# Output-gate block 4 between head 2's value tiles, and two branch projections behind the gates of block 2

## The chip, the core and the metric

One core of one Trainium2 chip runs the whole kernel in one launch. The metric is device time in microseconds, from the start of the program to its end. Engines are named as the profile names them: PE is TensorE (matmuls; PEld its weight loads), DVE is VectorE, ACT is ScalarE, POOL is GpSimd, SP is SyncE, which issues most of the DMAs.

## The reference, cut to what matters

The block is a residual layer on 512 tokens of width 1024 with two branches and a feed-forward part. What bears on the change:

```python
att = _forgetting_attention(fq, fk, fv, ff)              # 8 heads x 64
u  = silu(causal_conv(mu))                               # per channel, width 4
mq = einsum('bshi,hik->bshk', uh, w_mq)                  # 4 heads, qk 128
mk = einsum('bshi,hik->bshk', uh, w_mk)
hm = _mlstm_chunkwise(mq, mk, mv, mi, mf)                # v 256 for each head
hm = _head_norm(hm, mh_norm_g) * sigmoid(mo)
y  = sigmoid(ga) * (att @ w_pa) + sigmoid(gb) * (hm @ w_pb)
return y @ w_out
```

`mu`, `mv`, `mo`, `ga` and `gb` are column blocks of one input projection `h @ w_in + b_in`; `h` is the normalised and modulated input. Behind this come a LayerNorm, a SwiGLU feed-forward and a second LayerNorm.

## The kernel before

**Numbers.** Every fp32 product is made of three matmuls on fp32r halves (`mm3`, lines 184, 187 and 188): a value is split into `hi` (a cast on ACT, line 191) and `lo` (value minus `hi`, on DVE, line 192). Weights come in chunks in the order of `plan()`, are cast on ACT (line 155) and subtracted on DVE (line 159); `get(key)` asks for a chunk and starts the loads of the next three. Chunks pass through a ring of three raw buffers and a ring of four for the halves.

**Projections.** A block of 128 output columns, transposed, is 24 matmuls of 512 columns into one PSUM bank (`gemm_fm`); it is a generator that yields half-way and at its end. What empties the bank depends on the block: for `mo` a tanh on ACT (line 321) and a scaling on DVE (line 322) into a tile of the pool `mlb` for blocks 2 to 7; for `ga` and `gb` a tanh (line 583) into a tile of `mla` for block 0 and of `hml` for the others.

**PSUM.** Eight banks in four rings of two: `acc` (projections, value tiles, `mqk`), `s` (scores, `pa`, `pb`), `tr` (transposes), `o` (`fo` of the attention, `mn` of the mLSTM).

**The attention** (`fox_scores`, `fox_out`) runs over four pairs of heads. For each block `kb` of keys of a pair it transposes the weights (`ft`, line 661), ACT copies them out (`pT`, line 663), and `fo` (line 669) sums into a bank of the ring `o`; then `atthi` and `attlo` (lines 687, 688) empty it.

**The mLSTM** runs over four heads. `prep(h)` makes the values: four tiles of 128 tokens (`mv`, 24 matmuls of 256 columns each), each emptied by DVE into `vt` (line 612, one buffer) and split into `vxh` and `vx`; then `mqk`, from which queries and keys are copied. The tile `vxh` stands in a ring of two in the pool `adap`, tag `adaw`, which the loads of the modulation weights (`ada_load`) share. `ml_scores(h)` loads a row broadcast (`nb`, on ACT's queue, line 702), forms four weight tiles (E, line 707; a mask on POOL; the scores `ms`, line 710; a product on DVE, line 711; a split). `ml_num(h, tb)` sums `tb + 1` products into a bank of the ring `o` (`mn`, line 722), takes statistics and normalises into `hn` (lines 724 to 736). Two transposes per group (`mt`, line 755) fill two `tr` banks, and line 761 multiplies them with `mo` into `hm`.

**The order.** Work is written down in one sequence, and a planner at build time fixes each engine's order: earlier lines first, but what is ready by its own reckoning goes ahead of what isn't. A pool opened where another closed takes its memory, so its tiles wait for the old pool's last use: `mlb` is opened where `fox` closes (line 690), `hml` where `mlb` closes (line 763). Around the heads, `queue` holds generators (projections, `prep`), and `fill(n)` takes the next n steps of it. In the loop over heads, `fill(2)` stands behind the scores, `fill(1)` before each of the later groups, and two more at the last. A step is half a block, one value tile, or `mqk`.

**Behind the heads.** `hm` is split block by block into `hmhi` and `hmlo` (tiles of `hml`). Then, for f = 0 to 7: the gates `ga` and `gb` of block f (those of block 0 were made before), `pa` of block f (12 matmuls, emptied by line 792 into the gate's tile) and `pb_block(f - 1)` (24 matmuls on `hmhi` and `hmlo`, emptied by lines 778 and 780), whose result is split into `yhi` and `ylo`. From block 2 on, each gate projection is preceded by three `ada_block`s, a load and a reduction of modulation weights each.

Of the kernel before, what the change touches and what calls it, by code (L numbers as in the profile page):

```python
# [8 lines left out]
F32 = mybir.dt.float32  # L9
# [7 lines left out]
P = 128  # L17
D = 1024
S = 512
# [16 lines left out]
VW = TB * 258  # L36
# [6 lines left out]
def plan():  # L43
    out = [("start", k) for k in range(KT)]
    out += [("gv", j) for j in range(4)]

    def mu(h):
        return [("mu", 2 * h), ("mu", 2 * h + 1)]

    def mvqk(h):  # L50
        return [("mv", 2 * h), ("mv", 2 * h + 1), ("mqk", h)]

    out += mvqk(0)
    out += [("fq", 2), ("fk", 2)]
    out += mu(1) + mvqk(1)
    out += [("fq", 3), ("fk", 3)]
    out += mu(2)
    out += [("mo", 0), ("mo", 1)]
    out += mu(3)
    out += [("mo", 2), ("mo", 3)]  # L60
    out += mvqk(2)
    out += [("mo", 4), ("mo", 5)]
    out += mvqk(3)
    out += [("mo", 6), ("mo", 7)]
    for f in range(8):
        out += [("ga", f), ("gb", f), ("pa", f)]
        if f > 0:
            out += [("pb", f - 1)]
    out += [("pb", 7)]
    out += [("wo", k) for k in range(KT)]  # L70
    for f in range(FT):
        out += [("fg", f), ("fu", f)]
    for q in range(4):
        out += [("dn", q * 6 + j) for j in range(6)]
    return out
# [15 lines left out]


PLAN = plan()
POOL_LO = [("start", 0)]
LATE_LO = [(n, f) for f in range(3) for n in ("fg", "fu")]
# [3 lines left out]
def block_kernel(ctx, tc, x, c, wada, wpk, cols, gvb, mvb, lnp, out):  # L99
# [77 lines left out]
    def get(key, ahead=AHEAD):  # L177
        prefetch(key, ahead)
        return st["tiles"].pop(key)

    def mm3(ps, lhs, rhs, first, last, pin=False):
        lh, ll = lhs
        rh, rl = rhs
        m = T.matmul(ps, lh, rh, start=first, stop=False)  # L184
        if pin:
            tc.keep_in_program_order(m)
        T.matmul(ps, lh, rl, start=False, stop=False)  # L187
        T.matmul(ps, ll, rh, start=False, stop=last)  # L188

    def split(hi, lo, src):  # L190
        A.copy(hi, src)  # L191
        V.tensor_tensor(lo, src, hi.bitcast(F32), ALU.subtract)
# [27 lines left out]
    def scope(**kw):  # L220
        e = ExitStack()
        return e, e.enter_context(tc.tile_pool(**kw))
# [9 lines left out]
    ps = ctx.enter_context(tc.tile_pool(name="ps", bufs=2, space=PSUM))  # L232

    def acc_tile(name):
        return ps.tile([P, S], F32, tag="acc", name=name)

    def s_tile(name):
        return ps.tile([P, S], F32, tag="s", name=name)

    def tr_tile(name):  # L240
        return ps.tile([P, S], F32, tag="tr", name=name)
# [13 lines left out]
    ada_s, adap = scope(name="ada", bufs=2)  # L255
# [126 lines left out]
    for tb in range(TB):  # L382
        xt = xts[tb]
        mv = small.tile([P, 2], F32, tag="lnmv", name=f"xmv{tb}")
# [66 lines left out]
    def hk(k, sl=slice(0, S)):  # L451
        return hhi[:, k, sl], hlo[:, k, sl]

    def gemm_fm(name, b):
        hi, lo = get((name, b))
        if name in ("ga", "gb") and b > 1:
            for _ in range(3):
                ada_block()
        ps = acc_tile(f"{name}{b}")
        for k in range(KT):  # L460
            s_ = slice(k * P, (k + 1) * P)
            mm3(ps, (hi[:, s_], lo[:, s_]), hk(k), k == 0, k == KT - 1)
            if k in (3, KT - 1):
                yield
        gemm_done[(name, b)] = ps

    gemm_done = {}
    queue = []

    def fill(n):  # L470
        while n > 0 and queue:
            try:
                next(queue[0])
                n -= 1
            except StopIteration:
                queue.pop(0)

    def drain():
        fill(10 ** 6)
# [106 lines left out]
    def fm_unit(name, b):  # L586
        yield from gemm_fm(name, b)
        r = evac_fm(name, b, gemm_done.pop((name, b)))
        if name == "mo":
            mot[b] = r  # L590

    def prep_u(h):
        for i in range(2):
            b = 2 * h + i
            if b not in mup:
                yield from fm_unit("mu", b)
            conv(b)

    def prep(h):
        vl = mla.tile([P, TB, 258], F32R, tag="vx", name=f"vx{h}")  # L600
        vh = adap.tile([P, TB, 258], F32R, tag="adaw", name=f"vxh{h}", bufs=2)
        G.tensor_copy(vh[:, :, 256:258], ones[:, 0:2 * TB].rearrange("p (t o) -> p t o", o=2))
        G.tensor_copy(vl[:, :, 256:258], lfc[:, 0, 0:2 * TB].rearrange("p (t o) -> p t o", o=2))
        w0, w1 = get(("mv", 2 * h)), get(("mv", 2 * h + 1))
        for tb in range(TB):
            ps = acc_tile(f"mv{h}_{tb}")
            for k in range(KT):
                hi, lo = (w0, w1)[k // 4]
                s_ = slice((k % 4) * 256, (k % 4) * 256 + 256)
                mm3(ps[:, :256], hk(k, slice(tb * P, (tb + 1) * P)), (hi[:, s_], lo[:, s_]), k == 0, k == KT - 1)  # L610
            vt = mla.tile([P, 256], F32, tag="th", name=f"vt{h}_{tb}", bufs=1)
            V.tensor_tensor(vt, ps[:, :256], mvt[h // 2][:, (h % 2) * 256:(h % 2) * 256 + 256], ALU.add)
            split(vh[:, tb, 0:256], vl[:, tb, 0:256], vt)
            yield
        vx[h] = (vh, vl)
        hi, lo = get(("mqk", h))
        for i, dst in ((0, mq), (1, mk)):
            ps = acc_tile(f"mqk{h}_{i}")
            for k in range(2):
                s_ = slice((i * 2 + k) * P, (i * 2 + k + 1) * P)  # L620
                uh, ul = us[2 * h + k]
                mm3(ps, (hi[:, s_], lo[:, s_]), (uh, ul), k == 0, k == 1)
            t = mla.tile([P, S], F32, tag=f"qk{i}", name=f"qk{i}_{h}")
            A.copy(t, ps)
            dst[h] = t
        yield
# [109 lines left out]
        V.tensor_scalar(hn, po[:, 0:256], mv[:, 0:1], r[:, 1:2], ALU.subtract, ALU.mult)  # L736
        return hn

    queue += [fm_unit("mo", 2), fm_unit("mo", 3), prep(2), fm_unit("mo", 4), fm_unit("mo", 5)]
    queue += [prep_u(3), prep(3), fm_unit("mo", 6), fm_unit("mo", 7)]  # L740
    queue += [gate_unit("ga", 0), gate_unit("gb", 0)]
    for h in range(MH):
        while h not in mk:
            fill(1)
        Ws = ml_scores(h)
        fill(2)
        tr = [tr_tile(f"mt{h}_{i}") for i in range(2)]
        hn = ml_num(h, 0, Ws)
        for tb in range(TB):
            fill(1)  # L750
            nxt = ml_num(h, tb + 1, Ws) if tb + 1 < TB else None
            if nxt is None:
                fill(1)
            for i in range(2):
                T.transpose(tr[i][:, tb * P:(tb + 1) * P], hn[:, i * P:(i + 1) * P], ident)
            hn = nxt
        while 2 * h + 1 not in mot:
            fill(1)
        for i in range(2):
            b = 2 * h + i  # L760
            V.tensor_tensor(hm[:, b, :], tr[i], mot.pop(b), ALU.mult)
# [4 lines left out]
    hml_s, hml = scope(name="hml", bufs=1, side="right")  # L766
# [4 lines left out]
    def pb_block(f):  # L771
        pb = s_tile(f"pb{f}")
        hi, lo = get(("pb", f))
        for k in range(KT):
            s_ = slice(k * P, (k + 1) * P)
            mm3(pb, (hi[:, s_], lo[:, s_]), (hmhi[k], hmlo[k]), k == 0, k == KT - 1)
        tb_ = tbs.pop(f)
        V.scalar_tensor_tensor(tb_, tb_, 1.0, pb, ALU.add, ALU.mult)
        yt = tb_ if f > 0 else hml.tile([P, S], F32, tag="gb", name="y0", bufs=2)
        V.tensor_tensor(yt, tb_, tas.pop(f), ALU.add)  # L780
        return yt

    for f in range(KT):
        if f > 0:
            queue.extend([gate_unit("ga", f), gate_unit("gb", f)])
            drain()
        pa = s_tile(f"pa{f}")
        hi, lo = get(("pa", f))
        for k in range(4):
            s_ = slice(k * P, (k + 1) * P)  # L790
            mm3(pa, (hi[:, s_], lo[:, s_]), (atthi[:, k, :], attlo[:, k, :]), k == 0, k == 3)
        V.scalar_tensor_tensor(tas[f], tas[f], 1.0, pa, ALU.add, ALU.mult)
        if f > 0:
            yt = pb_block(f - 1)
            if f == 1:
                mla_s.close()
                y_s, yp = scope(name="yp", bufs=1)
                yp.tile([P, 48], F32, name="padY")
                yhi = yp.tile([P, KT, S], F32R, name="yhi")
                ylo = yp.tile([P, KT, S], F32R, name="ylo")  # L800
            split(yhi[:, f - 1, :], ylo[:, f - 1, :], yt)
    split(yhi[:, KT - 1, :], ylo[:, KT - 1, :], pb_block(KT - 1))

    while bg["e"] < 48:
# [458 lines left out]
```

## Time and profile before

| | |
|---|---|
| time, median of 3 runs | 861.1 us (858.8, 861.1, 861.79) |
| the profiled execution's own time | 860.83 us |
| its span, first to last instruction | 859.1 us |
| mean granted clock of PE | 0.995 |
| PE busy | 835.2 us (97%) |
| DVE busy | 596.4 us (69%) |
| ACT busy | 380.1 us (44%) |
| POOL busy | 81.0 us (9%) |

The time of an execution is its span and 1.73 us around it. Matmuls overlap a little in the profile (a row's duration is longer than the distance to the next row's start), so the cost of a matmul in a stream is read from starts.

### The profile page before, as it was taken

How to read it: one execution, taken by the hardware profiler on the slowest of the kernel's cores; microseconds unless marked ns; L12 is line 12 of the kernel's file. 1: busy time of each engine (PE TensorE's matmuls, PEld its weight loads, DVE VectorE, ACT ScalarE, POOL GpSimd, SP SyncE). 2: the span in 40 equal slices, each digit the busy share in tenths (PEclk: the TensorE clock that was granted, in tenths of full speed). 3: DMA queues.
4: the chain of work that ended last, by engine and by line, in shares of the span. 5: the costliest groups of instructions: out<-in, count | busy, mean ns of one | idle time of the engine just before them, and what ended most of it. 6: DMA issues, size and time to landing. Idle time of an engine off the chain costs nothing.

```text
span 859.1 us, 14123 instructions
## 1 busy us (share of the span) xinstructions
PE 835.2 (97%) x5518; PEld 749.3 (87%) x5518; DVE 596.4 (69%) x1113; ACT 380.1 (44%) x606; POOL 81.0 (9%) x140
## 2 busy tenths in 40 slices
PE   6999999999989999999999999999999999999996
PEld 4889877777779888888888899999999999999996
DVE  7968556554496668776656897877888878734247
ACT  5556767674453325232232365644445444612110
POOL 2030000000121110000000211111111110000001
PEclk9999999999999999999999999999999999999998
DMA  9953432421221225766677025678767774432202
GB/s 355 359 161 114 129 83 73 137 69 62 99 74 50 74 87 208 258 237 252 241 274 279 2 74 148 176 160 203 174 181 199 179 177 128 171 111 87 98 14 99
DMA packets 46477, 130.08 MB, mean 151 GB/s; under 512 B 5293, under 2 KB 5693, under 8 KB 46410
## 3 DMA queue, kind: packets, MB, share of 16 engines
q1 hardware_dynamic: 37930, 113.97, 38.5%
q0 software_dynamic: 6752, 12.06, 8.2%
q10 hardware_dynamic: 1728, 3.15, 1.3%
q8 instruction: 43, 0.70, 0.3%
q14 instruction: 24, 0.20, 0.1%
HBM read 124.93 MB, written 2.13 MB: 148 GB/s over the span
## 4 chain that ended last, share of the span: by engine, by line
PE 93%; DVE 2%; ACT 1%; issue 1%; DMA 0%; DVEq 0%; ACTq 0%
PE p L187 7%; PE p L184 7%; PE p L188 7%; PE dn L184 5%; PE dn L188 5%; PE dn L187 5%; PE mv L184 2%; PE mv L188 2%; PE mv L187 2%; PE mo L184 2%; PE mo L187 2%; PE gb L184 2%; PE ga L184 2%; PE ga L187 2%; PE ga L188 2%; PE pb L184 2%
## 5 line engine op out<-in xcount | busy, mean ns | idle before, releaser
L159 DVE TENSOR_TENSOR wlo<-raw,whi 128x1024 fp32r<-128x1024 f32 (+2 forms) x94 | 106.5, 1137 | 110.6 <-ACT whi L155 103.5
L155 ACT CAST whi<-raw 128x1024 fp32r<-128x1024 f32 (+2 forms) x98 | 95.4, 980 | 184.1 <-PE dn L188 72.9
L184 PE MATMUL dn<-whi,ah 128*128 128x256 f32 x352 | 98.0, 280 | 0.6 <-ACT ah L191 0.6
L187 PE MATMUL dn<-wlo,ah 128*128 128x256 f32 x352 | 97.7, 279 | 0.0
L188 PE MATMUL dn<-whi,al 128*128 128x256 f32 x352 | 96.5, 279 | 0.0
L187 PE MATMUL p<-tlo,whiu 128*128 128x256 f32 x304 | 84.9, 279 | 0.0
L184 PE MATMUL p<-thi,whiu 128*128 128x256 f32 x304 | 84.7, 279 | 0.1
L188 PE MATMUL p<-thi,wlou 128*128 128x256 f32 x304 | 84.6, 278 | 0.0
L184 PEld LDWEIGHTS dn<-whi,ah 128*128 128x128 f32 x352 | 66.0, 188 | 0.8 <-ACT ah L191 0.8
L187 PEld LDWEIGHTS dn<-wlo,ah 128*128 128x128 f32 x352 | 65.8, 187 | 0.0
L188 PEld LDWEIGHTS dn<-whi,al 128*128 128x128 f32 x352 | 65.5, 188 | 0.0
L184 PE MATMUL p<-hhi,whiu 128*128 128x256 f32 x228 | 63.6, 279 | 1.5 <-DVE at L1028 1.5
L187 PE MATMUL p<-hlo,whiu 128*128 128x256 f32 x228 | 63.7, 279 | 0.0
L188 PE MATMUL p<-hhi,wlou 128*128 128x256 f32 x228 | 63.5, 279 | 0.0
L269 DVE CUSTOM_DVE_ANT_0 adaw<-adaw,cb 128x1024 f32<-128x1024 f32 x32 | 39.1, 1223 | 26.4 <-DMA adaw<-in_wada_dram 26.1
L184 PEld LDWEIGHTS p<-thi,whiu 128*128 128x128 f32 x304 | 57.1, 188 | 0.3 <-ACT at L1027 0.3
L187 PEld LDWEIGHTS p<-tlo,whiu 128*128 128x128 f32 x304 | 57.1, 188 | 0.0
L188 PEld LDWEIGHTS p<-thi,wlou 128*128 128x128 f32 x304 | 56.9, 187 | 0.0
L184 PEld LDWEIGHTS p<-hhi,whiu 128*128 128x128 f32 x228 | 42.8, 188 | 1.7 <-issue 1.7
L208 POOL TENSOR_TENSOR lnrs<-lnrs,mhalf 128x1 f32<-128x1 f32 x12 | 13.1, 1094 | 325.8 <-DVE lnrs L207 325.8
L187 PEld LDWEIGHTS p<-hlo,whiu 128*128 128x128 f32 x228 | 42.8, 188 | 0.0
L188 PEld LDWEIGHTS p<-hhi,wlou 128*128 128x128 f32 x228 | 42.7, 187 | 0.0
(370 smaller groups left out, 2329.1 us busy)
## 6 DMA issues: line engine op xcount, KB each, us to landing
raw<-in_wpk_dram SPq DMA_DIRECT2D x84, 512.0 KB, 3.7
adaw<-in_wada_dram SPq DMA_DIRECT2D x48, 512.0 KB, 4.8
raws<-in_wpk_dram SPq DMA_DIRECT2D x57, 256.0 KB, 3.7
rawg<-in_wpk_dram SPq DMA_DIRECT2D x19, 512.0 KB, 3.9
raws<-in_wpk_dram POOLq DMA_DIRECT2D x38, 256.0 KB, 6.5
raw<-in_wpk_dram SPq DMA_DIRECT2D x16, 256.0 KB, 2.7
raw<-in_wpk_dram SPq DMA_DIRECT2D x8, 384.0 KB, 9.3
raw<-in_wpk_dram SPq DMA_DIRECT2D x4, 528.0 KB, 7.9
```

Source lines behind the costliest of these rows:

```text
L155: st["hi"] = A.copy(hi[:, :w], raw[:, :w])
L159: (G if key in POOL_LO else V).tensor_tensor(lo[:, :w], raw[:, :w], hi[:, :w].bitcast(F32), ALU.subtract)
L184: m = T.matmul(ps, lh, rh, start=first, stop=False)
L187: T.matmul(ps, lh, rl, start=False, stop=False)
L188: T.matmul(ps, ll, rh, start=False, stop=last)
L208: G.tensor_tensor(rs, rs, mhalf, ALU.pow)
L269: V.tensor_tensor_reduce(wt, wt, cb, 1.0, 0.0, ALU.mult, ALU.add, t)
```

## The change

Four edits. In the plan and the queue, block 4 of the output gate (`mo`, 4) leaves its place behind head 2's `mqk` and is made inside `prep(2)`, between its second and third value tile. Head 2's first value tile takes a bank of the ring `o` instead of `acc`. Behind head 0's scores five steps of the queue are taken instead of two. And `pb` of blocks 0 and 1 both come behind the gates and `pa` of block 2; the tile of `y0` is taken from the ring `adaw` instead of that of the `gb` gates.

```diff
--- before.py
+++ after.py
@@ -58,13 +58,14 @@
     out += [("mo", 0), ("mo", 1)]
     out += mu(3)
     out += [("mo", 2), ("mo", 3)]
-    out += mvqk(2)
-    out += [("mo", 4), ("mo", 5)]
+    out += [("mv", 4), ("mv", 5), ("mo", 4), ("mqk", 2), ("mo", 5)]
     out += mvqk(3)
     out += [("mo", 6), ("mo", 7)]
     for f in range(8):
         out += [("ga", f), ("gb", f), ("pa", f)]
-        if f > 0:
+        if f == 2:
+            out += [("pb", 0)]
+        if f > 1:
             out += [("pb", f - 1)]
     out += [("pb", 7)]
     out += [("wo", k) for k in range(KT)]
@@ -603,7 +604,8 @@
         w0, w1 = get(("mv", 2 * h)), get(("mv", 2 * h + 1))
         for tb in range(TB):
-            ps = acc_tile(f"mv{h}_{tb}")
+
+            ps = (o_tile if h == 2 and tb == 0 else acc_tile)(f"mv{h}_{tb}")
             for k in range(KT):
                 hi, lo = (w0, w1)[k // 4]
                 s_ = slice((k % 4) * 256, (k % 4) * 256 + 256)
@@ -612,6 +614,9 @@
             V.tensor_tensor(vt, ps[:, :256], mvt[h // 2][:, (h % 2) * 256:(h % 2) * 256 + 256], ALU.add)
             split(vh[:, tb, 0:256], vl[:, tb, 0:256], vt)
             yield
+            if h == 2 and tb == 1:
+
+                yield from fm_unit("mo", 4)
         vx[h] = (vh, vl)
@@ -736,14 +741,14 @@
-    queue += [fm_unit("mo", 2), fm_unit("mo", 3), prep(2), fm_unit("mo", 4), fm_unit("mo", 5)]
+    queue += [fm_unit("mo", 2), fm_unit("mo", 3), prep(2), fm_unit("mo", 5)]
     queue += [prep_u(3), prep(3), fm_unit("mo", 6), fm_unit("mo", 7)]
     queue += [gate_unit("ga", 0), gate_unit("gb", 0)]
     for h in range(MH):
         while h not in mk:
             fill(1)
         Ws = ml_scores(h)
-        fill(2)
+        fill(2 if h else 5)
         tr = [tr_tile(f"mt{h}_{i}") for i in range(2)]
@@ -776,7 +781,7 @@
         tb_ = tbs.pop(f)
         V.scalar_tensor_tensor(tb_, tb_, 1.0, pb, ALU.add, ALU.mult)
-        yt = tb_ if f > 0 else hml.tile([P, S], F32, tag="gb", name="y0", bufs=2)
+        yt = tb_ if f > 0 else adap.tile([P, VW], F32, tag="adaw", name="y0", bufs=2)[:, 0:S]
         V.tensor_tensor(yt, tb_, tas.pop(f), ALU.add)
         return yt
@@ -790,15 +795,16 @@
         V.scalar_tensor_tensor(tas[f], tas[f], 1.0, pa, ALU.add, ALU.mult)
-        if f > 0:
-            yt = pb_block(f - 1)
-            if f == 1:
+
+        for b in {0: (), 1: (), 2: (0, 1)}.get(f, (f - 1,)):
+            yt = pb_block(b)
+            if b == 0:
                 mla_s.close()
                 y_s, yp = scope(name="yp", bufs=1)
                 yp.tile([P, 48], F32, name="padY")
                 yhi = yp.tile([P, KT, S], F32R, name="yhi")
                 ylo = yp.tile([P, KT, S], F32R, name="ylo")
-            split(yhi[:, f - 1, :], ylo[:, f - 1, :], yt)
+            split(yhi[:, b, :], ylo[:, b, :], yt)
```

## Rows read from the trace of the kernel before

**Rows 1.** The page: busy time of the engines over the span.

```profile
PE 835.2 (97%) x5518; PEld 749.3 (87%) x5518; DVE 596.4 (69%) x1113; ACT 380.1 (44%) x606; POOL 81.0 (9%) x140
```

**Rows 2.** PE's waits from 190 to 262 us: total, times, longest.

```profile
PE mv L184 <- DVE vt L612: 2.4, 1, 2.4
PE mv L184 <- ACT mo L321: 1.8, 1, 1.8
```

**Rows 3.** Windows: length, busy time by engine, granted clock, DMA share, GB/s.

```profile
243.25:455.20 211.95, 211.95 (x1046) 178.61 (x1047) 150.63 (x336) 72.96 (x107) 10.88 (x24) 1.00 0.52 185
...
225.05:228.46 3.41, 3.41 (x19) 3.41 (x18) 0.00 (x0) 0.43 (x1) 0.00 (x0) 0.51 0.81 304
```

**Rows 4.** PE's timeline at the end of the attention: start, duration, line, operation.

```profile
220.69 0.33 PE L661 MATMUL ft<-ident,L 128*128 128x128 f32 x1
...
221.53 0.44 PE L669 MATMUL fo<-pT,v 128*64 128x128 f32 x4 [0.28 <-ACT pT L663]
223.78 0.39 PE L184 MATMUL mv<-whi,hhi 128*128 128x256 f32 x1 [1.81 <-ACT mo L321]
...
231.23 0.37 PE L184 MATMUL mn<-vxh,Eh 128*128 128x258 f32 x1
```

**Rows 5.** ACT's timeline from the end of the attention on.

```profile
222.02 0.58 ACT L687 CAST atthi<-fo 128x512 fp32r<-128x512 f32 x1 [0.54 <-PE fo L669]
...
223.05 0.69 ACT L321 ACTIVATE mo<-mo,halfc 128x512 f32<-128x512 f32 x1 [0.44 <-ACT atthi L687]
...
228.03 1.23 ACT L707 ACTIVATE E<-nb,gc 128x512 f32<-128x512 f32 x2 [3.71 <-DMA nb<-rowd]
```

**Rows 6.** PE's timeline around head 2's last value tile and the blocks behind it.

```profile
239.91 0.28 PE L188 MATMUL mn<-vxh,El 128*128 128x258 f32 x1
...
243.25 0.39 PE L184 MATMUL mv<-whi,hhi 128*128 128x256 f32 x1 [2.41 <-DVE vt L612]
...
246.09 0.38 PE L755 MATMUL mt<-ident,hn 128*128 128x128 f32 x2
...
249.02 0.40 PE L184 MATMUL mqk<-uhi,whi 128*128 128x512 f32 x1
...
250.43 0.40 PE L184 MATMUL mo<-hhi,whi 128*128 128x512 f32 x1
...
261.34 0.38 PE L755 MATMUL mt<-ident,hn 128*128 128x128 f32 x2
```

**Rows 7.** DVE's timeline over the same stretch.

```profile
241.79 0.41 DVE L192 TENSOR_TENSOR vx<-vt,vxh 128x256 fp32r<-128x256 f32 x1
...
242.78 0.42 DVE L612 TENSOR_TENSOR vt<-mv,mvt 128x256 f32<-128x256 f32 x1
...
249.08 0.42 DVE L612 TENSOR_TENSOR vt<-mv,mvt 128x256 f32<-128x256 f32 x1
```

**Rows 8.** The page's DMA issues: weight chunks, KB each, us to landing.

```profile
raw<-in_wpk_dram SPq DMA_DIRECT2D x84, 512.0 KB, 3.7
```

**Rows 9.** PE's timeline at the end of the attention's pair 2.

```profile
181.56 0.33 PE L661 MATMUL ft<-ident,L 128*128 128x128 f32 x1
...
186.52 0.44 PE L669 MATMUL fo<-pT,v 128*64 128x128 f32 x4
```

**Rows 10.** PE's timeline over head 3's groups and up to the first `pb`.

```profile
301.41 0.40 PE L184 MATMUL ga<-hhi,whi 128*128 128x512 f32 x1
...
304.90 0.40 PE L184 MATMUL gb<-hhi,whi 128*128 128x512 f32 x1
...
323.33 0.38 PE L755 MATMUL mt<-ident,hn 128*128 128x128 f32 x2
...
330.15 0.39 PE L184 MATMUL pb<-hmhi,whi 128*128 128x512 f32 x1
```

**Rows 11.** ACT's timeline behind head 3.

```profile
325.37 4.27 ACT L191 CAST hmhi<-hm 128x512 fp32r<-128x512 f32 x8 [2.57 <-DVE hm L761]
329.55 0.68 ACT L583 ACTIVATE tga<-ga,halfc 128x512 f32<-128x512 f32 x1
```

## The prediction

> **What bounds the kernel now.** I read the page first: TensorE (PE) is busy for 97% of the span [rows 1], so only what removes idle or slowed time of PE can shorten it; no work is taken out here. Then the list of PE's waits around head 2's value tiles: two long ones, 1.8 us for the tanh of an output-gate block and 2.4 us for `vt` [rows 2]. Then the windows: after the first wait PE runs 3.41 us at a granted clock of 0.51 (1.2 GHz instead of 2.4), and from 243.25 to 455.2 us it is busy for all of 211.95 us [rows 3]. So what the early parts of the change can win lies between 221 and 243 us, and what they can lose lies behind it, where today no wait shows. Last the timelines, engine by engine, for what each wait hangs on.
>
> I write v0 to v3 for head 2's value tiles (`prep(2)`), n0 to n3 for the four `ml_num` groups of a head, pa1, ga1, gb1 and so on for blocks of the projections.
>
> *First wait.* The last `fo` of fox pair 3 starts at 221.53, v0 at 223.78 after 1.81 us of idling [rows 4]. Both banks of the `acc` ring hold mo2 and mo3. Their tanh writes into `mlb`, which is opened where `fox` closes, so it can't run before the last `fo`: ACT casts `atthi` at 222.02 and starts the tanh at 223.05 [rows 5]. The `nb` load for head 0's weights is gated likewise; the first E activation waits for it until 228.03 [rows 5], and n0 starts at 231.23 [rows 4].
>
> *Second wait.* The last matmul of n3 of head 0 starts at 239.91; v3 at 243.25, after 2.41 us idle [rows 6]. `vxh` of head 2 takes the ring slot of head 0's, which n3 reads. So after n3 come the split (`vx` at 241.79) and then `vt` of v1 at 242.78, for there is one `vt` buffer [rows 7]; that frees the bank for v3. This is a chain of 243.25 - 239.91 = 3.3 us, of which PE covers some with a `ms` quad.
>
> **The change, part by part.** *Prices.* 48 `mo` matmuls run from 250.43 to 261.34, so one block of 24 takes 5.46 us and one matmul 0.2275 us; v3's 24 run from 243.25 to 246.09, 2.84 us [rows 6]. mo4 keeps its 24 matmuls, its tanh, its DVE step and its 512 KB chunk (3.7 us from issue to landing [rows 8]); the chunk swaps places with `mqk2`'s on SP's queue. It takes the freed weight slot of mo2 rather than mo3's, so it is in place before v1 ends. Cost 0; the three chunks of prefetch hide it, and if they didn't, it would cost up to that 3.7 us.
>
> *v0 in the `o` ring.* Its bank is free (pair 2's `fo` was evacuated long before), so v0 need not wait for mo2. But the program's order on PE is fixed ahead by the planner, which pulls any ready lower work into the gaps of the fox tail. At the same place of pair 2, between the last `ft` (181.56) and the last `fo` (186.52), 4.96 us, stand 19 matmuls of `mo` and three of scores [rows 9]. In pair 3 that gap holds one `mo` matmul, because both `acc` banks are used up: 220.69 to 221.53 [rows 4]. With a bank of its own v0 is what fits there: 24 short matmuls, about 12 long ones' worth. They go ahead of the last `fo`, which then moves from 221.53 by 2.84 less the 0.28 us that PE idles before it [rows 4], and a little overlap: about 2.4 us. Everything gated by the end of fox moves with it: `nb`, mo2's tanh, and v1, which still wants an `acc` bank. The 1.8 us wait then stands before v1 instead of v0.
> Bounds: if v0 goes wholly behind the last `fo`, that end doesn't move (shift 0); if all of it goes ahead, 2.4 us. I take 2.4, for the row of pair 2 is nearest.
>
> *mo4 between v1 and v2.* It uses the `acc` bank that mo3's tanh frees, and its own tanh frees that bank again for v2: a ring gives out whichever bank is free. The row that shows this is `mqk2`'s second half, which starts at 249.02 [rows 6] while v3's `vt` only starts at 249.08 [rows 7]; so it took the bank of the first half. Thus 5.46 us of PE work stand in front of n2, n3 and v2, and v2's rest covers the 3.3 us chain after n3. The time of v3 is set by chains: end of fox, `nb`, E, n0 to n3, `vt`. It moves by the 2.4 us of above, while mo4 is then already done. Gain by v3: 5.46 - 2.4 = 3.1 us. Bounds: 5.5 with no shift; 0.3 if v2 still has to wait for `vt` of v1 (3.1 less v2's 2.84).
> The slowed 3.41 us count for nothing in this sum: they ended at 228.46, while the E work that n0 needs only began at 228.03 [rows 5].
> Less filler stands behind v3 (mo5 alone), but the order then brings v0 and v1 of head 3 ahead of n2 and n3 of head 1, 5.7 us for the 5.46 taken. Cost 0.
>
> *fill(5).* The queue now runs three units ahead of the heads. Before, the 26 units (half a block or a value tile each) were spread so that head 3's groups still had gb0 and half of ga0 between them; now they are used up ahead of head 3's n0. What is left to fill its chain is pa0, ga1, gb1, pa1 and, since pb0 has moved, pa2: 12 + 24 + 24 + 12 + 12 = 84 matmuls. Today 67 matmuls of fill (24 of gb0, 12, 24 and 7) stand between the end of n1 at 304.90 and the last transposes at 323.33 [rows 10], placed there by the planner for the same chain. 84 - 67 = 17 would stand behind those transposes, 3.9 us.
> What must pass there: today PE has 29 matmuls until 330.15 [rows 10]; meanwhile `hm` is formed, ACT makes eight casts from 325.37, and only then, at 329.55, comes the tanh of ga1 (0.68 us) [rows 11] that gives back a bank. From the end of the transposes (323.71) to 330.23 that is 6.5 us. ga2 needs this bank; pb0, too, finds both `s` banks held by pa1 and pa2, whose evacuations need that tanh and ga2's. Behind ga2 on PE stand gb2, pb0, pb1 and all that follows, so nothing hides it: PE waits 6.5 - 3.9 = 2.6 us where it waits 0 now. Bounds: 0 if 29 or more are left, 6.5 if none is.
>
> *pb0 and pb1 behind ga2, gb2, pa2.* 48 matmuls, their four DVE steps and two splits, and two chunks on SP's queue, all moved and none added. The move puts pa2 into the hole, counted above. `y0` takes a slot of the ring of the `adaw` loads for some us; SP's later loads stand behind it, with weights three chunks ahead and DMA at a share of 0.52 there [rows 3]. Cost 0; without that cover some 3.7 us once [rows 8].
>
> *Sum*: 860.83 us (span 859.1, and 1.73 around it) - 3.1 + 2.6 = 860.3 us. The median of the three runs, 861.1, is 0.03% above that execution; runs spread from 858.8 to 861.79, so 0.3% (2.6 us) is about the least that can be told from no change.
>
> **The clock.** After the 1.81 us wait the clock fell to the lower level, after the 2.41 us wait it didn't (the stretch from 243.25 runs at 1.00 [rows 3]). So I give a fall half a chance wherever the tail waits; the sum has none, and if the clock falls, 3.41 us at 0.51 lose 1.7 us. The Trainium skill (TensorE: Matmul & The Clock Gate, Why this matters for your kernels) says to leave no idle gaps between bursts of matmuls, or the clock drops to its lower level. By that rule, reading this wait as such a gap, the sum would be 862.0 us; the trace bears it out in one of these two waits.
>
> **Rivals.**
> *The tail is covered* (chance 0.22). If head 3's chain, with no unit forced between its groups, takes 55 matmuls or fewer, 29 stay behind the transposes as now. For it: 24 of today's 67, those of gb0, stand there by program order, whether the chain needs them or not. Against: gb0 ends exactly where n2 begins, so n2 may have needed all of it. Time 860.83 - 3.1 = 857.7, faster.
> *The first wait goes* (0.13). v0 stays behind the last `fo`. Against it: pair 2's gap. 860.83 - 5.5 + 2.6 = 857.9, or 855.3 with the tail covered; faster.
> *The tail bursts* (0.22), the other side. Head 3's chain takes 84 matmuls of fill or more, so that none is left behind the transposes: PE waits the whole 6.5 us, and the clock falls half the time. 860.83 - 3.1 + 6.5 = 864.2, with the fall 865.9; slower. It decides from a loss of 5.7 us on, that is with fewer than 4 matmuls left, or fewer than 11 and the fall. For it: today 12 matmuls of ga0, from 301.41 on, stand between n0 and n1 [rows 10]; if that gap stays and is filled, 5 of the 17 are left and the wait is 5.4 us.
> *It doesn't do what it says* (0.08): v2 waits for `vt` as v3 did. 860.83 - 0.3 + 2.6 = 863.1, same, on the edge of slower.
> *The forecast* (0.35): v0 ahead of `fo`, gain 3.1, tail wait 1 to 4.5 us: 858.7 to 862.2, and 863.9 with the fall; mostly no difference.
>
> **Numbers.** Predicted 860.3 us. The range takes the first three rivals in down to 857 and up to 865; outside are the best of the second (855.3) and the worst of the third. Faster by over 0.3%: 0.22 + 0.13 and 0.02 of the forecast's lower edge, 0.37. Slower: 0.18 of the third, 0.03 of the fourth, 0.02 of the forecast, 0.23. Same: 0.40.
>
> **What would show it.** In the profile after: v0's matmuls between the last `ft` and the last `fo` (if behind it, my shift is wrong); a wait of about 1.8 us for L321 before v1; no wait for `vt` before v3; mo4 ahead of n2; and PE idle some 2 to 3 us before ga2, waiting for the tanh of L583, soon after head 3's last transposes. The prediction is wrong if that last wait is missing or above 5 us, or if a new wait shows in heads 1 and 2, where I have put none.

## The result and the profile after

| | before | after |
|---|---|---|
| median of 8 runs | 861.11 us (855.09 to 863.16) | 865.97 us (864.27 to 871.73) |
| profiled execution, and its span | 860.83 / 859.1 us | 868.96 / 867.2 us |

The ratio is 1.0075, with an interval of 1.0051 to 1.0099: slower by 0.75%, and 865.97 us is just above the predicted range of 857 to 865. Behind the projections PE runs the same matmuls at two rates, and what sets the rate is not known (last section); the traces differ there by several us. So kernels are compared below by medians, and traces by the time from one lone `mo` matmul just ahead of the last `fo` of the attention (220.77 us before, 220.32 after) to the first matmul of `wo` (455.41 and 464.62). That stretch was 234.64 us before and is 244.30 now: 9.7 us longer. The trace is of one execution of each kernel. PE's work is the same; the page's busy line of after:

```profile
PE 835.2 (96%) x5518; PEld 748.6 (86%) x5518; DVE 596.2 (69%) x1113; ACT 380.0 (44%) x606; POOL 81.7 (9%) x140
```

PE's waits from 180 to 470 us in after (compare [rows 2]). A new one of 9.8 us stands at their head:

```profile
PE ga L185 <- ACT tga L584: 9.8, 1, 9.8
PE mv L185 <- DVE vt L614: 1.8, 1, 1.8
PE mv L185 <- ACT mo L322: 1.3, 1, 1.3
```

The stretch cut at v3's start, at the end of head 3's last transposes, at ga2's start and after it (windows, columns as in [rows 3]):

```profile
220.32:245.94 25.62, 22.32 (x149) 19.35 (x149) 16.88 (x57) 12.82 (x27) 4.79 (x15) 1.00 0.26 83
245.94:330.37 84.43, 84.43 (x482) 73.01 (x482) 60.79 (x182) 30.56 (x50) 11.25 (x21) 1.00 0.34 109
330.37:340.15 9.78, 0.00 (x1) 0.00 (x0) 8.69 (x16) 5.52 (x11) 0.00 (x0) 0.67 0.39 144
340.15:350.40 10.25, 10.25 (x37) 8.36 (x38) 4.61 (x7) 2.16 (x3) 0.00 (x0) 0.81 0.01 2
350.40:464.62 114.22, 114.22 (x508) 94.45 (x506) 74.11 (x129) 32.47 (x42) 0.00 (x0) 1.00 0.71 248
```

Only the third and fourth rows are new in kind. In the third PE does nothing: it waits first for DVE, which makes `hm` only at 333.89, then for ACT's casts of it and the tanh of ga1. In the fourth PE is busy throughout, but at a granted clock of 0.81: 37 matmuls at 0.2275 us would take 8.42 us, so 1.8 us are lost.

*Early.* From the lone `mo` to v3 it was 243.25 - 220.77 = 22.48 us and is 25.62, with mo4's 5.46 us now inside: 5.46 - 3.14 = 2.3 us won. Half of that is idle time: 22.48 less 17.98 us busy, or 4.5 us, before and 25.62 less 22.32, or 3.3 us, now. The other half is PE's clock, which fell behind the first wait in the kernel before [rows 3] and not here. The end of the attention, on PE's timeline:

```profile
220.63 0.28 PE L185 MATMUL mv<-whi,hhi 128*128 128x256 f32 x1
...
223.20 0.44 PE L674 MATMUL fo<-pT,v 128*64 128x128 f32 x4
223.57 0.38 PE L185 MATMUL mv<-whi,hhi 128*128 128x256 f32 x1
...
225.44 0.38 PE L185 MATMUL mv<-whi,hhi 128*128 128x256 f32 x1 [1.25 <-ACT mo L322]
```

Of v0's 24 matmuls 21 stand ahead of the last `fo`, as forecast, and the first wait stands before v1.

*Late.* PE behind head 3's last transposes, DVE around them, and ACT behind them:

```profile
329.99 0.38 PE L760 MATMUL mt<-ident,hn 128*128 128x128 f32 x2
340.15 0.79 PE L185 MATMUL ga<-hhi,whi 128*128 128x512 f32 x1 [9.78 <-ACT tga L584]
340.75 0.63 PE L188 MATMUL ga<-hlo,whi 128*128 128x512 f32 x1
341.17 0.63 PE L189 MATMUL ga<-hhi,wlo 128*128 128x512 f32 x1
```

```profile
318.95 1.23 DVE L270 CUSTOM_DVE_ANT_0 adaw<-adaw,cb 128x1024 f32<-128x1024 f32 x1 [0.85 <-DMA adaw<-in_wada_dram]
...
322.23 1.22 DVE L270 CUSTOM_DVE_ANT_0 adaw<-adaw,cb 128x1024 f32<-128x1024 f32 x1
...
324.95 1.23 DVE L270 CUSTOM_DVE_ANT_0 adaw<-adaw,cb 128x1024 f32<-128x1024 f32 x1 [0.64 <-DMA adaw<-in_wada_dram]
...
327.48 0.54 DVE L741 TENSOR_SCALAR hn<-mn,mmv,mr 128x256 f32<-128x256 f32 x1
328.09 1.23 DVE L270 CUSTOM_DVE_ANT_0 adaw<-adaw,cb 128x1024 f32<-128x1024 f32 x1
...
331.46 1.22 DVE L270 CUSTOM_DVE_ANT_0 adaw<-adaw,cb 128x1024 f32<-128x1024 f32 x1 [2.14 <-DMA adaw<-in_wada_dram]
...
333.89 1.28 DVE L766 TENSOR_TENSOR hm<-mt,mo 128x512 f32<-128x512 f32 x2
```

```profile
335.26 4.26 ACT L192 CAST hmhi<-hm 128x512 fp32r<-128x512 f32 x8 [4.26 <-DVE hm L766]
339.42 0.68 ACT L584 ACTIVATE tga<-ga,halfc 128x512 f32<-128x512 f32 x1
```

DVE at the same place in the kernel before:

```profile
318.46 0.55 DVE L736 TENSOR_SCALAR hn<-mn,mmv,mr 128x256 f32<-128x256 f32 x1
...
323.98 1.28 DVE L761 TENSOR_TENSOR hm<-mt,mo 128x512 f32<-128x512 f32 x2
...
329.04 1.22 DVE L269 CUSTOM_DVE_ANT_0 adaw<-adaw,cb 128x1024 f32<-128x1024 f32 x1
```

Two things are to be seen. Nothing stands between the transposes and ga2: all 84 matmuls of fill are used up in front. And the reductions of modulation weights that belong to the gates of block 2 (L270, 1.22 us each, with idle time for their loads) now stand between the steps that make `hn` and `hm`, where before the first of them came at 329.04, behind `hm`. DVE runs them in the order that the planner fixed, so `hn` of n3 starts 8.7 us behind n3's end (318.78), and `hm` starts 3.5 us after the transposes, where it started within 0.3 us before (323.98 against 323.71).

### The profile page after: what moved, and what is told of

Same layout as the page of the kernel before. It is cut to its first block, busy times and chain, and to the rows that moved or that the text cites. A ratio compares the mean times of both kernels' runs of the same rounds, so it can differ in the third digit from the quotient of the medians.

```text
span 867.2 us, 14125 instructions
## 1 busy us (share of the span) xinstructions
PE 835.2 (96%) x5518; PEld 748.6 (86%) x5518; DVE 596.2 (69%) x1113; ACT 380.0 (44%) x606; POOL 81.7 (9%) x140
## 4 chain that ended last, share of the span: by engine, by line
PE 90%; DVE 3%; DMA 2%; ACT 2%; issue 1%; SPq 0%; DVEq 0%; ACTq 0%
PE p L185 7%; PE p L189 7%; PE p L188 7%; PE dn L185 5%; PE dn L189 5%; PE dn L188 5%; PE mv L185 2%; DMA adaw<-in_wada_dram 2%; PE mo L189 2%; PE mo L185 2%; PE mo L188 2%; PE pb L189 2%; PE pb L185 2%; PE mv L189 2%; PE pb L188 2%; PE mv L188 2%
## 5 line engine op out<-in xcount | busy, mean ns | idle before, releaser
L270 DVE CUSTOM_DVE_ANT_0 adaw<-adaw,cb 128x1024 f32<-128x1024 f32 x32 | 39.1, 1223 | 25.9 <-DMA adaw<-in_wada_dram 25.7
```

What stands on the lines that cost most here:

```text
L270: V.tensor_tensor_reduce(wt, wt, cb, 1.0, 0.0, ALU.mult, ALU.add, t)
```

## The experiments

Three theories went in. A: drawing five units at head 0 uses up all the fill ahead of head 3's last transposes, and block 2's reductions then stand in `hn`'s and `hm`'s way on DVE. B: the moved `pb` blocks are to blame by themselves. C: the early part is, with v0 ahead of the last `fo`.

"mo to wo" is the stretch defined above, from the profiled execution. The ratios are to runs of the kernel before beside each kernel (medians 861.1 to 862.0 us); they are not the quotients of the medians.

| kernel | median, us | ratio and interval | mo to wo, us |
|---|---|---|---|
| before | 861.1 | | 234.64 |
| after | 866.0 | 1.0075 [1.0051, 1.0099] | 244.30 |
| e1_pb_back | 866.0 | 1.0027 [1.0004, 1.0049] | 239.74 |
| e2_pb_only | 862.9 | 1.0012 [1.0000, 1.0025] | 236.07 |
| e3_ada_later | 871.8 | 1.0111 [1.0096, 1.0127] | 244.67 |
| e4_fill2 | 863.1 | 1.0014 [1.0005, 1.0022] | 236.39 |
| b_fill5 | 868.5 | 1.0089 [1.0057, 1.0121] | 241.05 |
| v0_behind | 869.5 | 1.0087 [1.0057, 1.0117] | 244.33 |
| g5111 | 859.2 | 0.9968 [0.9938, 0.9998] | 232.46 |
| g5111_pbb | 859.0 | 0.9981 [0.9956, 1.0007] | 232.40 |
| b_5111 | 861.9 | 1.0003 [0.9973, 1.0032] | 234.78 |
| g5111_pbb_acc | 858.3 | 0.9943 [0.9922, 0.9964] | 231.71 |
| f2_pbb_acc | 856.0 | 0.9954 [0.9925, 0.9982] | 231.85 |
| b_o | 865.9 | 1.0054 [1.0023, 1.0085] | 239.23 |

**The pb blocks put back (e1_pb_back).** To after:

```diff
-        if f == 2:
-            out += [("pb", 0)]
-        if f > 1:
+        if f > 0:
             out += [("pb", f - 1)]
...
-        for b in {0: (), 1: (), 2: (0, 1)}.get(f, (f - 1,)):
+        for b in (f - 1,) if f > 0 else ():
...
-        yt = tb_ if f > 0 else adap.tile([P, VW], F32, tag="adaw", name="y0", bufs=2)[:, 0:S]
+        yt = tb_ if f > 0 else hml.tile([P, S], F32, tag="gb", name="y0", bufs=2)
```

> The change with pb0 and pb1 put back to where they were (pb0 behind pa1, y0 in its old ring); mo4, the o ring for v0 and fill(5) stay. Theory A (fill(5) takes all the fill in front of head 3's last transposes, and block 2's ada reductions then stand ahead of hm on DVE): still nothing is left behind the transposes, but the work that comes first is now pb0, which needs hm, one cast and one hmlo and no bank from the tanh, so PE waits 3 to 5 us for hmlo instead of 9.8 for the tanh: 860 to 862.5 us, no difference from before. Theory B (moving pb0 and pb1 is to blame by itself, since it puts pa2 into the hole): the wait is gone and the 2.8 us of the early part show: about 858.3 us. Theory C (the early part, with v0 ahead of the last fo, is what costs): 865 us or more, as with the whole change.

Its two waits behind head 3 (list of waits):

```profile
PE pb L183 <- ACT hmhi L190: 3.2, 1, 3.2
PE pb L186 <- DVE hmlo L191: 1.1, 1, 1.1
```

They come to 4.2 us, as theory A has it, and B falls, since the waits and the loss stay with `pb` back. But the matmuls behind them were slow too (9 of pb0 in 4.01 us, from 332.47 to 336.48, instead of 2.05), which the expectation left out: 866.0 us, above A's range. By the time alone C, with its 865 us or more, would have held; the later runs decide between them. Mo to wo is 4.6 us shorter than in the change and 5.1 longer than before.

**The pb move alone (e2_pb_only).** The same lines, the other way, on the kernel before.

> The kernel before with the move of pb0 and pb1 alone (y0 in the adaw ring); mo4, v0's bank and fill(2) as before. Theory A: gb0's last 17 matmuls and pa1 still stand behind the last transposes, 29 matmuls or 6.6 us, which is the length of the chain through hm, the casts and ga1's tanh: PE waits 0 to 1 us before ga2, 860.5 to 862.5 us, the same as before. Theory B: a wait of several us before ga2 and 864 us or more. Theory C: 861 us, no wait.

Measured 862.9 us, with one small new wait:

```profile
PE ga L186 <- ACT tga L585: 1.2, 1, 1.2
```

29 matmuls stand behind the transposes, and the chain to the tanh took 1.2 us more than they do. So the move alone costs about a microsecond (0.9 us in the medians, 1.4 by mo to wo); B is out as the main cause.

**The reductions one block later (e3_ada_later).** To after:

```diff
-        if name in ("ga", "gb") and b > 1:
+        if name in ("ga", "gb") and b > 2:
```

> The whole change, but the ada reductions of two blocks begin with gate block 3 instead of gate block 2, and two more of them are done at the end instead. Theory A: hm is formed right behind head 3's transposes, one half of pa2's fill (12 matmuls, 2.7 us) stands behind them by the program's order, and the wait before ga2 falls from 9.8 to 3 to 5 us; without the long wait the half clock behind it may go as well (1.8 us): 857.5 to 861.5 us. Theory B (the pb move alone): the bank for ga2 still comes from the same tanh at the same place, the wait stays at 6.5 us or more: 863 us or more. Theory C: 865 us or more, since the early part is untouched.

The wait before ga2 fell from 9.8 to 3.5 us, as A has it, and another took its place (list of waits, then DVE's timeline at head 3's end and at the end of the `pb` blocks):

```profile
PE pb L185 <- DVE tga L797: 5.2, 1, 5.2
PE ga L185 <- ACT tga L584: 3.5, 1, 3.5
```

```profile
323.33 0.54 DVE L741 TENSOR_SCALAR hn<-mn,mmv,mr 128x256 f32<-128x256 f32 x1
...
328.39 1.29 DVE L766 TENSOR_TENSOR hm<-mt,mo 128x512 f32<-128x512 f32 x2 [1.97 <-PE mt L760]
...
456.94 1.23 DVE L270 CUSTOM_DVE_ANT_0 adaw<-adaw,cb 128x1024 f32<-128x1024 f32 x1 [3.70 <-DMA adaw<-in_wada_dram]
```

Without the reductions `hn` of n3 starts 3.7 us behind n3's end (319.59), twelve matmuls (2.7 us) are left behind the transposes, and `hm` starts as the transposes end (328.39 and 328.46). 2.7 + 3.5 = 6.2 us is the chain that the prediction sized at 6.5. But the reductions and their loads now crowd the end of the gates: the evacuation of the last `pa` stands behind one that waits 3.7 us for its load, and PE waits 5.2 us for it. I expected 857.5 to 861.5 us and got 871.8, where C's time lies; the part of the wait that the reductions make is shown all the same.

**The whole change with fill(2) (e4_fill2).** To after:

```diff
-        fill(2 if h else 5)
+        fill(2)
```

> The whole change, but with fill(2) ahead of head 0 as before. Theory A: the queue is back in step, 29 matmuls stand behind the last transposes, PE waits 0 to 1.5 us before ga2, and mo4 still stands ahead of v3, so most of the 2.8 us of the early part is kept: 857.5 to 860.5 us, faster than before by 0.1 to 0.4%. Theory B: a wait of several us before ga2 remains, 863 us or more. Theory C: as v1 now comes first and v0 is behind the last fo, the first wait changes its place, and the time goes back to 861 us or below.

Measured 863.1 us, above A's 857.5 to 860.5. The tail is as A expects (1.3 us before ga2, with 29 matmuls or 6.6 us of fill behind the transposes). The early gain is not: with less drawn, v1 goes first behind the last `fo` after the old 1.8 us wait, v0 comes only behind n2, and v3 still waits 1.3 us for `vt`.

**Fill(5) alone (b_fill5).** To the kernel before:

```diff
-        fill(2)
+        fill(2 if h else 5)
```

> The kernel before with fill(5) ahead of head 0 and nothing else of the change. Theory A: no fill is left behind head 3's last transposes, two ada reductions stand ahead of hm on DVE, and PE waits for hm's casts and hmlo as with pb put back: some 4 us in all and a stretch at half clock behind it, with nothing won early: 864 to 869 us, slower by 0.3 to 0.8%. Theory B (the pb move) and theory C (mo4 and v0): fill(5) alone costs nothing, 861 to 863 us.

868.5 us; mo to wo is 6.4 us longer than before, with these waits behind head 3 and a granted clock of 0.68 over the 5.4 us from the first of them on:

```profile
PE pb L184 <- ACT hmhi L191: 3.0, 1, 3.0
PE pb L187 <- DVE hmlo L192: 1.2, 1, 1.2
```

That is theory A with nothing else of the change, and 868.5 us lies in its range.

**v0 held behind the last fo (v0_behind).** To after (`fo` is the last matmul of the attention, `after` an order on PE alone):

```diff
-                mm3(ps[:, :256], hk(k, slice(tb * P, (tb + 1) * P)), (hi[:, s_], lo[:, s_]), k == 0, k == KT - 1)
+                mm3(ps[:, :256], hk(k, slice(tb * P, (tb + 1) * P)), (hi[:, s_], lo[:, s_]), k == 0, k == KT - 1,
+                    behind=st["fo"] if h == 2 and tb == k == 0 else None)
...
+        if behind is not None:
+            after(m, behind)
```

> The whole change, but v0's first matmul is held behind the last fo by an order on PE alone; it keeps the o ring's bank. By the prediction's step (v0 ahead of fo delays the end of fox by 2.4 us and with it nb, the tanh of mo2 and v3): the last fo goes back by 2.4 us, v0 covers the first wait, and v3 comes 2 us or more earlier. The rival: PE's work is only reordered, so that what v0 no longer takes ahead of fo it takes behind it; then only the 1.25 us wait before v1 can go, and v3 comes 0 to 1.3 us earlier. The tail is that of the change in both, with its wait of about 9.8 us. So 863 to 864 us by the one and 864.5 to 866 us by the other.

With v0 held back, the last `fo` and n0 came 2.3 and 2.4 us earlier, counted from the lone `mo` at 220.91 (after: 223.20 and 233.30):

```profile
221.51 0.44 PE L676 MATMUL fo<-pT,v 128*64 128x128 f32 x4
...
231.45 0.37 PE L185 MATMUL mn<-vxh,Eh 128*128 128x258 f32 x1
```

So the shift that the prediction forecast is there. But v3 came only 0.3 us earlier: PE waited 0.9 and 1.8 us for `hn` instead. The tail wait was 8.7 us, and mo to wo is the change's (244.33). The rival was right about the early part; the median, 869.5 us, is above what either gave, and in its ratio not to be told from the change.

**The same change with the fill spread 5, 1, 1, 1 (g5111, g5111_pbb).**

```diff
-        fill(2 if h else 5)
+        fill((5, 1, 1, 1)[h])
```

The second also has the `pb` lines of e1_pb_back.

> The whole change, but with fill(5), fill(1), fill(1), fill(1) ahead of heads 0 to 3, so that head 0 draws as much as in the change and head 3 is back in step with the kernel before (eight units in all). Theory A (the change loses because the units drawn early are missing behind head 3's last transposes): the early part is that of the change (v0 ahead of the last fo, v3 at about 246, 2.8 us won), and 6 matmuls of gb1 and 24 of pa1 and pa2, 30 or 6.8 us, stand behind the last transposes. The chain there is 6.5 us, up to 3 more where block 2's ada reductions stand ahead of hm on DVE: PE waits 0 to 2.5 us before ga2, 858.5 to 861.5 us, at least 4 less than the whole change. Theory B (the moved pb blocks cost by themselves): 862.5 us or more. Theory C (v0 ahead of fo, and the early part): 865 us or more.

> As the last kernel, and with pb0 and pb1 back where they were. Theory A: 10 matmuls of gb1 and 12 of pa1 (5.0 us) stand behind the last transposes and pb0 after them, which needs only hm, the first cast and hmlo; no ada reduction stands ahead of hm. The wait there is 0 to 1 us, and the 2.8 us of the early part show: 858.5 to 860.5 us, faster than before by 0.2 to 0.4%. Theory B: the same time or better than the kernel with pb moved by some us. Theory C: no gain, 861 us or more.

PE behind head 3's last transposes in the first of them, and its DVE:

```profile
323.07 0.38 PE L760 MATMUL mt<-ident,hn 128*128 128x128 f32 x2
323.20 0.47 PE L185 MATMUL gb<-hhi,whi 128*128 128x512 f32 x1
...
330.13 0.43 PE L185 MATMUL ga<-hhi,whi 128*128 128x512 f32 x1
```

```profile
323.71 1.28 DVE L766 TENSOR_TENSOR hm<-mt,mo 128x512 f32<-128x512 f32 x2
```

Thirty matmuls stand between the transposes and ga2, no wait and no fall of the clock follows, and mo to wo is 11.8 us shorter than in the change, only because eight units are drawn behind the four heads' scores and not eleven. Reductions stand ahead of `hm` here too, but with thirty matmuls behind the transposes they cost nothing. Moving `pb` is worth nothing here, either way (232.46 and 232.40). Theory A holds; C is out, for the early part is the change's.

**The fill spread alone (b_5111).** To the kernel before:

```diff
-        fill(2)
+        fill((5, 1, 1, 1)[h])
```

> The kernel before with fill(5), fill(1), fill(1), fill(1) ahead of heads 0 to 3 and nothing else of the change. It parts the gain of the last two kernels: if the spread of the units alone wins it, this one comes to 858.5 to 860.5 us. Theory A: the gain is that of mo4 ahead of v3, with v0 in its own bank; here both waits (1.8 and 2.4 us) and the half clock after the first stay, head 3's tail is covered, and the time is that of before, 860.5 to 862.5 us.

861.9 us: nothing is won, and v3's 2.4 us wait is there.

**The better version without v0's bank (g5111_pbb_acc).** To g5111_pbb:

```diff
-            ps = (o_tile if h == 2 and tb == 0 else acc_tile)(f"mv{h}_{tb}")
+            ps = acc_tile(f"mv{h}_{tb}")
```

> The better version (fills 5, 1, 1, 1 and pb0, pb1 where they were) with v0 back in the acc ring, so that of the change only mo4's place is left. By the prediction's step for mo4 (its 5.46 us stand ahead of n2, n3 and v2, and v2 covers the chain through vt), v3 comes without a wait and 2 to 3 us are won even so: 858.5 to 860 us. Theory A: with both acc banks held by v0 and v1, whose vt stands behind n3's split, it is v2 that now waits some 2.4 us behind n3 where v3 did, mo4 has only taken v2's old place, and the first wait of 1.8 us with its half clock stays: 860.5 to 862.5 us. So it tells whether v0's bank is needed for the gain.

858.3 us, and mo to wo is 0.7 us shorter than with the bank. Theory A had said too much here: the bank isn't needed, and the prediction's step for mo4 was right.

**mo4's move alone (f2_pbb_acc).** To the kernel before:

```diff
-    out += mvqk(2)
-    out += [("mo", 4), ("mo", 5)]
+    out += [("mv", 4), ("mv", 5), ("mo", 4), ("mqk", 2), ("mo", 5)]
...
+            if h == 2 and tb == 1:
+                yield from fm_unit("mo", 4)
...
-    queue += [fm_unit("mo", 2), fm_unit("mo", 3), prep(2), fm_unit("mo", 4), fm_unit("mo", 5)]
+    queue += [fm_unit("mo", 2), fm_unit("mo", 3), prep(2), fm_unit("mo", 5)]
```

**v0's bank alone (b_o).** To the kernel before:

```diff
-            ps = acc_tile(f"mv{h}_{tb}")
+            ps = (o_tile if h == 2 and tb == 0 else acc_tile)(f"mv{h}_{tb}")
```

> The kernel before with mo4 moved between v1 and v2 and nothing else (v0 in the acc ring, fill(2) for every head, pb0 and pb1 where they were). Theory A2 (mo4's place alone is the gain; the spread of the units only has to leave 27 to 29 matmuls behind head 3's last transposes): the first wait of 1.8 us stays, v3 has no wait, the tail is that of before and waits for nothing, and the first projection of the output weights starts 2.5 to 3 us earlier than before: 857.5 to 859.5 us. The rival (the fills 5, 1, 1, 1 are needed for it, as fill(5) was for v0 ahead of the last fo): the wait for vt comes back at v2 or v3 and the time is 860.5 to 862 us.

> The kernel before with v0 in the o ring's bank and nothing else. Theory A2: no gain in it by itself. As with the whole change at fill(2), v1 goes first behind the last fo and still waits 1.8 us for the tanh of mo2, and the wait for vt stays before v3: 861 to 863.5 us. The rival (a bank of its own for v0 takes the first wait away): 859 to 860 us.

mo4's place alone gives the whole gain: 856.0 us, 0.9954, and 2.8 us by mo to wo. Of these, 1.7 us are idle time and 1.1 us the clock, which did not fall behind the first wait in this execution. It did not fall in b_5111's either (1.00 from 223.55 to 230.00), and there PE waited 1.2 us more than in the kernel before and nothing was won; so the fall alone does not make the difference. Its waits from 190 to 262 us, and PE around n3's end:

```profile
PE mv L183 <- ACT mo L320: 1.8, 1, 1.8
PE ms L713 <- DVE E L714: 0.8, 1, 0.8
```

```profile
242.06 0.28 PE L187 MATMUL mn<-vxh,El 128*128 128x258 f32 x1
242.18 0.81 PE L713 MATMUL ms<-qk,qk 128*128 128x256 f32 x4
242.75 0.37 PE L183 MATMUL mv<-whi,hhi 128*128 128x256 f32 x1
```

v2 starts without a wait behind n3 (it takes the bank that mo4 left) and v3 behind v2. v0's bank alone is a loss, 865.9 us, more than either theory gave (the profiled execution is its fastest, 857.43 us, with mo to wo 4.6 us longer than before):

```profile
PE mt L755 <- DVE hn L736: 2.3, 1, 2.3
PE mv L184 <- ACT mo L321: 1.8, 1, 1.8
PE mv L184 <- DVE vt L612: 1.3, 1, 1.3
PE ms L710 <- DVE E L711: 1.1, 1, 1.1
```

There v1 and v2 go ahead and v0 is left for later, so nothing stands behind n1 to hide the normalisation. That v0 is the one left is read from the waits: the tile that comes first waits for a bank of `acc`. The one edit, mo4's, on the kernel before beats both kernels.

## Why the prediction was wrong

*v0 ahead of the last `fo`, first wait to v1.* Right: 21 of 24 matmuls, and 1.25 us where 1.8 was forecast. The last `fo` came 0.76 us behind the lone `mo` before and 2.88 in the change, a shift of 2.1 us for the 2.4 forecast; against v0_behind it is 2.3.

*Gain by v3, 3.1 us.* Measured 2.3. The size was near and the reason only half right. It was written as 5.46 less the shift of the attention's end; by that a kernel without the shift should win 5.5 us. The kernel with mo4's move alone has no shift and won 2.8, the one with v0 held back hardly more by v3 than the change (0.3 us). What can be won here is PE's idle and slowed time, whatever stands where: the waits of [rows 2] are 4.2 us together, the slowed stretch some 1.7, and no kernel won more than 2.9 us by `wo`. Nor did v3's wait go wholly in the change: 1.84 us of it stayed, against the forecast.

*mo4's place, and v2 covering the chain behind n3.* Right in f2_pbb_acc, where v2 and v3 stand behind n3 and neither waits. Not in the change: there v2 ran ahead of n2 and n3, from 237.85, and covered nothing, which is why v3 waited.

*pb0 and pb1 moved, cost 0 but for pa2 in the hole.* Nearly: 1.2 us of wait alone, nothing where 30 matmuls are left.

*The tail, the step that failed.* It said: "84 - 67 = 17 would stand behind those transposes", and a chain of 6.5 us against those. None stood there, and the chain was 9.8 us, above the 5 us at which the prediction called itself wrong. The two errors go back to one cause, as far as e3_ada_later shows it. From the fill behind n1 to the last transposes it was 18.4 us before (304.90 to 323.33) and is 22.3 (307.71 to 329.99): 3.9 us more, just the 17 matmuls that I had counted on. Behind them another 3.3 us. With the reductions out of the way (e3_ada_later) twelve were left and the wait was 3.5 us: the step's method, near its numbers (17 and 2.6), would have held. I had followed what fill(5) does to PE's order and not what happens in DVE's: the reductions that go ahead of block 2's gates moved in front of `hm`, into the chain that the fill was to cover. Without the move of `pb` the effect is there too (b_fill5: 4.2 us of waits).

*The clock.* Forecast at half a chance and 1.7 us; it fell and cost 1.8. The Trainium skill (TensorE: Matmul & The Clock Gate, Why this matters for your kernels) advises against idle gaps between bursts of matmuls, since the clock drops to its lower level; for the 9.8 us gap the trace agrees (0.81 in the stretch behind it).

In sum the change is the rival "the tail bursts". That its fall price, 865.9 us, is next to the 865.97 measured is luck. By the traces the terms are others: -2.3 early, +9.8 of wait, +1.8 of clock, 9.3 of the 9.7 us. And of these 9.7 us the medians show 4.9. The eight runs of the change fall into five from 864.27 to 865.99, the profiled one at 868.96, and two at 871.63 and 871.73; the two lie about 10 us above the kernel before. That the five were faster behind `wo`, by the second rate of the last section, is likely, but they have no trace.

## What to carry to other kernels

Work drawn early to fill one gap is missing in a later one: count the fill behind the last chain, and look on every engine's queue for what the drawn work brings with it, here reductions on DVE that lengthened the very chain. Try the edits of a bundle one by one: here one of four won 0.3 to 0.5% and two of the others lost more than that. And a reordering that takes no work out wins at most idle or slowed time of the engine that bounds the kernel, so size it by the waits, not by the work that was moved.

## What the hardware showed beside this

The clock's answer to a wait of one length at one place is not fixed. Before the first value tile PE waited 1.81 or 1.82 us in several kernels; behind it the granted clock was at 0.75 over the next 6.8 us in the kernel before and 0.66 over 4.3 us in e4_fill2, but 1.00 in b_fill5 and f2_pbb_acc. Behind the 3.5 us wait of e3_ada_later it was 0.77.

In the feed-forward part PE runs the same matmuls at two rates, both at a granted clock of 1.00 and without idle time. Windows of 20 us, the kernel before and then mo4's move alone:

```profile
600.00:620.00 20.00, 20.00 (x172) 20.00 (x172) 16.25 (x22) 9.03 (x13) 3.49 (x4) 1.00 0.76 182
```

```profile
600.00:620.00 20.00, 20.00 (x179) 20.00 (x178) 18.30 (x26) 10.80 (x14) 3.85 (x5) 1.00 0.81 213
```

It is 4% more matmuls in the second. In that profiled execution the higher rate lasts from 540 to 720 us, in the one of after from about 555 to 610, and in the one of before only from about 550 to 575; what sets it, these runs do not show. The stretch behind `wo` is the shorter the longer it lasts: the kernel before took 403.7 us, mo4's move alone 398.2, and v0's bank alone, which has it from about 550 to 690 us and again from 740, 396.0 with the same work. That it is also why the runs of one kernel spread over some 8 us is likely but not shown, for each kernel has one trace. It is why the traces were compared up to `wo`. So of its 0.46% only the 2.8 us ahead of `wo` (0.33%) are traced to the edit; whether the rest is chance stays open.
